# adaLN matrices of a hybrid layer: eight feature blocks summed by VectorE with the input loaded first, instead of two of them by TensorE

## The chip, the core and the metric

The kernel is written for a Trainium2 chip and runs on one of its cores. A core has a matrix engine (TensorE, PE in the profile; PEld is its weight load), VectorE (DVE), ScalarE (ACT), GpSimd (POOL) and SyncE (SP), each with its own queue of instructions that it works off in order. They work on an on-chip memory of 128 partitions; TensorE writes into accumulation banks. Transfers are issued from the queues of SyncE and ScalarE and carried by 16 DMA engines. The metric is the time of one execution on the device in microseconds (us), as the median over several runs. Engines wait for each other and for transfers by semaphores, and a transfer's semaphore is one of eight that are used in turn, so a transfer is issued once the one eight places earlier has landed.

## The reference

The model layer takes x of 2048 tokens by 1024 features and one condition vector c of 1024. What matters here is the start:

```
c_act = silu(c)
mod = c_act @ w_ada + b_ada                  # 1024 -> 6 x 1024
shift_m, scale_m, gate_m, shift_f, scale_f, gate_f = split(mod, 6)
h = rms_norm(x, g_norm_mix) * (1 + scale_m) + shift_m
p = h @ w_in                                 # 1024 -> 3592
...                                          # convolutions, gated delta rule, w_out, feed-forward, final adaLN
```

So the first projection needs, for each feature, a shift and a scale, each the dot product of c_act with a column of w_ada, and x normalised along its rows. Everything is in float32.

## The kernel before, in words

The kernel works through the 2048 tokens in four blocks of 512 (BLK), and features are split into eight feature blocks of 128 (KD). Activations stand with features on the partitions, so x is normalised token by token and then turned by TensorE transposes. To keep float32 precision, an operand of a projection is split into a high part (a cast to the fast float32 type) and a low part (the difference); a product is then three matmuls, high by high, low by high and high by low. For the weights, ScalarE makes the high part `whi` (L368) and VectorE the low part `wlo` (L370); for the activations ScalarE scales the transposed block with the per-feature scale Gm and shift Sm (L509) and casts it to `hTh` (L510), and VectorE makes `hTl` (L511).

The head, before the loop over token blocks, does this for the first 512 tokens (tiles kq, four x tiles of 128 tokens) and feature block by feature block, k = 0 to 7. For each block it needs Gm and Sm of 128 features, that is two times 128 dot products of length 1024. There are two ways in the kernel before, chosen by `AHEAD = 2`:

- Blocks 0 and 1: a separately laid out copy `w_first` of those columns is loaded with the 1024 inputs on partitions, and TensorE multiplies it with c as a column (tile `cs`, in the storage of Gf; loaded by a small transfer of its own and put through Silu): eight matmuls of one output column for each of shift and scale, L776, accumulated in a bank.
- Blocks 2 to 7: the matrix is loaded transposed, features on partitions, and VectorE multiplies each row with the broadcast row of c (tile `crow`, shown as gate_m) and sums along the row in one instruction, L439, twice per block (scale first, then shift), into columns of two small tiles `totals` (shown as ms).

Either way ScalarE then makes Gm (L782) and Sm (L783). The matrices of the blocks lie in four places, kd, vt, yah and zs, in turn, so block k + 4 is loaded when block k is summed. Beside this the head loads and splits five weight strips of w_in (four in the ring `wraw` of four buffers, the fifth in `yal`), and projects each block with all strips that are there, so that five strips are projected at the end of the head.

The order on each engine isn't the order of the program text. A planner (class Clock) records each instruction with a cost of its own and a start time, and at the end pins, engine by engine, the instructions in the order of those planned times. Small pieces of side work are released by the same planned clock. A change in the head can therefore move instructions on any engine and anywhere behind it.

Of the kernel before, what the change touches and what calls it, by code (L numbers as in the profile page):

```python
# [12 lines left out]
F32 = mybir.dt.float32  # L13
F32R = mybir.dt.float32r
AF = mybir.ActivationFunctionType
# [5 lines left out]
P = 128  # L21
D = 1024
S = 2048
KD = D // P
# [6 lines left out]
CH = BLK // P  # L31
# [180 lines left out]


@with_exitstack
def layer_kernel(ctx, tc, x, c, w_ada, c_col, w_first, cols, g_norm_final, w_in, w_ab, xt, a_log, dt_bias, w_out, w_gate_up,
                 w_down, cst, out):
    nc = tc.nc
    x, out = x[0], out[0]
    w_down = w_down[0]
    mm = nc.tensor.matmul  # L220
# [16 lines left out]
    def misc_ps():  # L237
        return pm.tile([P, 512], F32, name="pm")
# [105 lines left out]
    epsc = g0.tile([P, 1], F32, name="epsc")  # L344
# [6 lines left out]
    col, at = {}, 0  # L351
# [3 lines left out]
    gb = g0.tile([P, KD], F32, name="gb")  # L355
# [51 lines left out]
    reqs, ready, bg = requests(), deque(), deque()  # L407
# [30 lines left out]
    def sums_of(raw, row, total):  # L438
        nc.vector.scalar_tensor_tensor(raw, raw, 1.0, row, op0=ALU.mult, op1=ALU.mult, accum_out=total)  # L439
# [80 lines left out]
    Gm, Sm, Gf, Sf = (g0.tile([P, KD], F32, name=n) for n in ("Gm", "Sm", "Gf", "Sf"))  # L520
# [146 lines left out]
    with ExitStack() as actx:  # L667
        ap_ = Split(rctx, actx, {"hTh", "hTl", "kq", "kd", "vt", "zs", "E", "X", "lv", "ch", "Dg", "state"},
                    {"halo0", "halo1", "rs", "uhalo0", "uhalo1", "edge", "uedge", "et", "strict_r", "gones_r", "junkd", "nk", "nq", "sk",
                     "bk", "rq", "cb", "ab2", "sp_y", "sp_n", "sp_e", "sp_s", "sp_z", "sp_p", "g", "beta",  # L670
                     "g_hi", "g_lo", "eg", "so"})
# [66 lines left out]
        totals = [g0.tile([P, KD], F32, name="ms", bufs=2) for _ in range(2)]  # L738
# [8 lines left out]
        crow = ap_.tile([P, D], F32, name="gate_m")  # L747
        PLACES = ("kd", "vt", "yah", "zs")

        def x_load(i):  # L750
            nc.sync.dma_start(xt0[i], x[i * P:(i + 1) * P, :])
# [7 lines left out]
                    nc.scalar.activation(xt0[i - 1], xt0[i - 1], AF.Identity, scale=ss[i - 1])  # L759

        def ada_load(k):
            if k < AHEAD:
                t = ap_.tile([P, 2, KD, P], F32, name=PLACES[k % 4])
                nc.sync.dma_start(t, w_first[k])
            else:
                t = ap_.tile([P, 2, D], F32, name=PLACES[k % 4])
                nc.sync.dma_start(t, w_ada[0:2, k].rearrange("s p n -> p s n"))
            return t

        def ada_sums(k, raw):  # L770
            if k < AHEAD:
                ps = misc_ps()
                sums = [ps[:, s:s + 1] for s in range(2)]
                for s in (1, 0):
                    for i in range(KD):
                        mm(sums[s], raw[:, s, i, :], cs[:, i:i + 1], start=s == 1 and i == 0, stop=i == KD - 1,  # L776
                           skip_group_check=True)
# [4 lines left out]
            nc.scalar.activation(Gm[:, k:k + 1], sums[1], AF.Identity, scale=col["g_mix"][:, k:k + 1], bias=gb[:, k:k + 1])  # L782
            nc.scalar.activation(Sm[:, k:k + 1], sums[0], AF.Identity, bias=col["b_sm"][:, k:k + 1])  # L783

        def proj_ab(ps, ks):
            for k in ks:
# [15 lines left out]
        nc.scalar.activation(crow, crow, AF.Silu)  # L802
# [12 lines left out]
        x_norm()  # L815
        wab = g0.tile([P, KD, 8], F32, name="wab")
        nc.sync.dma_start(wab, w_ab)
# [6 lines left out]
        for k in range(KD):  # L824
            ada_sums(k, raws[k])
            ps = turned
# [36 lines left out]
        for b in range(NB):  # L863
# [389 lines left out]
            for key, c0, dstT in (("k", 2048, kT), ("q", 1536, qT), ("v", 2560, None)):  # L1253
                clock.pinned = clock.pinned or key == "k"
                for h in range(NH):
                    m = (c0 - 1536) // P + h
                    if pre:
                        w, ps = pre.pop(0)
# [3 lines left out]
                    else:  # L1262
                        w, ps = next_w(), dense_ps()
# [22 lines left out]
            for h in range(NH):  # L1286
                w = next_w()
                ps = dense_ps()
# [67 lines left out]
            for g, group in enumerate(out_groups(b)):  # L1356
                pso = {}
                for i, (n, kp, ts) in enumerate(group):
# [132 lines left out]
    jobs, sums = deque(), deque()  # L1491
# [14 lines left out]
    strips = [(hf, m) for hf in range(2) for m in range(NF)]  # L1506
    raws, Ws, acts = {}, {}, {}
# [114 lines left out]
    raw, x0 = ready.popleft()  # L1622
# [36 lines left out]
    raws, acts_d = {}, {}  # L1659
# [211 lines left out]
    for n, (g, s) in enumerate(items):  # L1871
# [9 lines left out]
        if g == 0:  # L1881
            for q in range(4):
                p = dense_ps()
# [58 lines left out]
def laid_out(v):  # L1942
    f = {n: np.asarray(a) for n, a in v.items()}
    given = {n: f[n] for n in ("x", "c")}
    ada = np.concatenate([f["w_ada"][0], f["w_ada_final"]], axis=1)
    given["w_ada"] = ada.T.reshape(8, KD, P, D)
    given["c_col"] = f["c"].reshape(KD, P).T
    given["w_first"] = ada[:, :2 * D].reshape(KD, P, 2, KD, P)[:, :, :, :AHEAD].transpose(3, 1, 2, 0, 4)
# [31 lines left out]
```

## Time and profile before

| | us |
|---|---|
| median of three runs | 2390.36 (2387.8 to 2390.41) |
| the profiled execution, its time | 2392.24 |
| its span, first to last instruction | 2390.5 |
| TensorE busy | 2324.8 (97%) |
| VectorE busy | 1739.2 (73%) |
| ScalarE busy | 1069.5 (45%) |

In the lines of the profile, a group of instructions reads: line of the kernel, engine, operation, output tile <- input tiles with their shapes, number, then busy time, mean of one in ns, and the idle time of the engine just before them with what ended it. A row of the timeline begins with its start and its duration in us. A row of the chain of waits has start, length and what filled it; the chain is followed back from the last instruction, at each step to what released it. A row of the table by stages has the stage, its length, the busy time (and number of records) of PE, PEld, DVE, ACT and POOL, the granted TensorE clock, the share of the DMA engines and GB/s. One float32 matmul of full precision, as in L776, shows as two records.

### The profile page before, as it was taken

The numbers are of one execution on the slowest core, as the hardware profiler recorded it, in microseconds if no ns is written. First come the engines' busy times: TensorE is split into PE (matmuls) and PEld (weight loads), VectorE is DVE, ScalarE is ACT, GpSimd is POOL, SyncE is SP. The second block draws the span as 40 slices with busy tenths as digits, with TensorE's granted clock in tenths as the row PEclk, the third lists the DMA queues.
The fourth block names the chain that finished last, engine by engine and source line by source line (L and its number), as shares of the span: only waits on it lengthen the run. The fifth ranks groups of instructions, "written<-read, shape, count | busy, mean of one in ns | idle before, by whom it ended". The sixth has DMA issues, their size and how long they took to land.

```text
span 2390.5 us, 30803 instructions
## 1 busy us (share of the span) xinstructions
PE 2324.8 (97%) x11167; PEld 1924.3 (81%) x11167; DVE 1739.2 (73%) x2673; ACT 1069.5 (45%) x1865; POOL 596.8 (25%) x651
## 2 busy tenths in 40 slices
PE   6999999999999999999999999999999999999997
PEld 5788778888888888887878888878888887888786
DVE  3788859785978678786665556875655668878887
ACT  4734566445744474366433334433333323322345
POOL 0331444135413461201000000000000035434447
PEclk9999999999999999999999999999999999999999
DMA  7344555534463536255753334763433374333333
GB/s 271 106 139 123 172 177 167 164 98 163 131 209 117 178 111 203 63 167 168 231 187 103 113 89 146 233 185 93 119 97 102 106 252 150 124 106 125 131 132 149
DMA packets 217842, 352.45 MB, mean 147 GB/s; under 512 B 39149, under 2 KB 131609, under 8 KB 217370
## 3 DMA queue, kind: packets, MB, share of 16 engines
q1 hardware_dynamic: 215816, 347.46, 46.2%
q0 software_dynamic: 1152, 2.10, 0.7%
q8 instruction: 87, 1.43, 0.2%
q10 hardware_dynamic: 722, 0.93, 0.1%
q14 instruction: 65, 0.53, 0.1%
HBM read 277.01 MB, written 75.52 MB: 147 GB/s over the span
## 4 chain that ended last, share of the span: by engine, by line
PE 76%; DVE 9%; DMA 6%; ACT 4%; issue 3%; POOL 2%; SPq 0%; ACTq 0%; DVEq 0%; POOLq 0%
PE pd L325 49%; PE pm L325 17%; DVE wlo L370 1%; DVE acc L1814 1%; DMA y<-xT 1%; DVE cv L1231 1%; DMA y<-in_w_ada_dram 1%; POOL wraw L1743 1%; PE pm L898 1%; DMA A12d<-y 1%; PE pm L1113 1%; PE pm L1073 1%; PE pm L1065 1%; PE pm L1179 1%; PE pm L1187 1%
## 5 line engine op out<-in xcount | busy, mean ns | idle before, releaser
L368 ACT CAST whi<-wraw 128x1024 fp32r<-128x1024 f32 x285 | 298.5, 1049 | 368.5 <-PE pd L325 164.2
L370 DVE TENSOR_TENSOR wlo<-wraw,whi 128x1024 fp32r<-128x1024 f32 x285 | 368.4, 1294 | 119.2 <-ACT whi L368 117.5
L325 PE MATMUL pd<-hTh,whi 128*128 128x512 f32 x888 | 363.9, 410 | 6.4 <-DVE edge L1268 3.0
L325 PE MATMUL pd<-hTh,wlo 128*128 128x512 f32 x888 | 349.2, 393 | 0.0
L325 PE MATMUL pd<-hTl,whi 128*128 128x512 f32 x888 | 349.1, 393 | 0.0
L325 PEld LDWEIGHTS pd<-hTh,whi 128*128 128x128 f32 x888 | 168.3, 190 | 40.0 <-issue 3.4
L1608 POOL TENSOR_TENSOR wraw<-wraw 128x1024 f32<-128x1024 f32 x2 | 5.3, 2659 | 781.5 <-DMA wraw<-in_w_down_dram 781.5
L325 PEld LDWEIGHTS pd<-hTh,wlo 128*128 128x128 f32 x888 | 168.1, 189 | 37.1 <-issue 0.2
L325 PEld LDWEIGHTS pd<-hTl,whi 128*128 128x128 f32 x888 | 168.7, 190 | 29.4
L1231 DVE SCALAR_TENSOR_TENSOR cv<-pd,pc,cv 128x511 f32<-128x511 f32 (+2 forms) x173 | 129.1, 746 | 41.7 <-ACT cv L1229 37.9
L1556 DVE TENSOR_TENSOR sg<-sg,pd 128x512 f32<-128x512 f32 x44 | 30.2, 686 | 171.9 <-PE pd L325 171.4
L1814 DVE TENSOR_TENSOR acc<-acc,pd 128x512 f32<-128x512 f32 x192 | 127.4, 679 | 24.7 <-PE pd L325 24.6
L1694 ACT CAST xh<-ra 128x640 fp32r<-128x640 f32 (+1 forms) x85 | 60.4, 721 | 183.8 <-PE pm L325 134.4
L1703 POOL TENSOR_TENSOR xl<-ra,xh 128x640 fp32r<-128x640 f32 (+1 forms) x37 | 62.5, 1688 | 143.9 <-ACT xh L1694 143.1
L1814 DVE TENSOR_TENSOR acc<-acc,pm 128x512 f32<-128x512 f32 x120 | 81.7, 681 | 19.3 <-PE pm L325 18.8
L1743 POOL TENSOR_TENSOR wraw<-wraw 128x512 f32<-128x512 f32 x40 | 69.1, 1750 | 48.7 <-DMA wraw<-in_w_down_dram 41.7
L325 PE MATMUL pd<-whi,ym 128*128 128x512 f32 x256 | 80.4, 390 | 0.0
L325 PE MATMUL pd<-A22h,whi 128*128 128x512 f32 x176 | 70.3, 400 | 6.8 <-DVE sg L1556 6.8
L1313 DVE RECIPROCAL cv<-cv 128x128 f32<-128x128 f32 x64 | 57.1, 926 | 22.3 <-ACT cv L1310 22.2
L325 PE MATMUL pm<-S1h,whi 128*128 128x512 f32 x176 | 69.2, 393 | 1.8 <-ACT whi L368 1.8
L325 PE MATMUL pm<-S1h,wlo 128*128 128x512 f32 x176 | 69.3, 394 | 0.5 <-DVE wlo L370 0.5
L325 PE MATMUL pd<-A22l,whi 128*128 128x512 f32 x176 | 69.8, 396 | 0.0
(450 smaller groups left out, 6195.5 us busy)
## 6 DMA issues: line engine op xcount, KB each, us to landing
wraw<-in_w_in_dram SPq DMA_DIRECT2D x112, 512.0 KB, 4.4
wraw<-in_w_gate_up_dram SPq DMA_DIRECT2D x88, 512.0 KB, 3.7
ra<-act SPq DMA_DIRECT2D x80, 448.0 KB, 3.6
wraw<-in_w_out_dram SPq DMA_DIRECT2D x40, 512.0 KB, 3.7
act<-S SPq DMA_DIRECT2D x80, 256.0 KB, 2.7
act<-act SPq DMA_DIRECT2D x68, 256.0 KB, 2.2
wraw<-in_w_ada_dram SPq DMA_DIRECT2D x32, 512.0 KB, 4.3
cb<-in_x_dram SPq DMA_DIRECT2D x48, 256.0 KB, 3.7
```

The source lines that it names most:

```text
L325: mm(*args, **kw)
L368: nc.scalar.copy(hi, raw)
L370: (lo_engines.popleft() if lo_engines else nc.vector).tensor_sub(lo, raw, hi.bitcast(F32))
L898: nc.tensor.transpose(ps[:, j * P:(j + 1) * P], src[:, j * P:(j + 1) * P], ident)
L1065: mm(py[:, j * P:(j + 1) * P], Mm[h][:, j, :], T[h][:, j, :], start=True, stop=True)
L1231: nc.vector.scalar_tensor_tensor(cv[:, n - t:], u[:, :BLK - n + t], taps[t], cv[:, n - t:], op0=ALU.mult, op1=ALU.add)
L1313: nc.vector.reciprocal(sy[:, qs], sy[:, qs])
L1556: nc.vector.tensor_add(s5[i], s5[i], a[i])
L1694: nc.scalar.copy(hi, raw[:, c0:c1, :])
L1703: eng.tensor_sub(lo, raw, hi.bitcast(F32))
L1743: nc.gpsimd.tensor_mul(r[:, hs], r[:, hs], gate_f[:, hs])
L1814: nc.vector.tensor_add(accs[s, u][:, ns], accs[s, u][:, ns], ps)
```

## The change

All eight feature blocks now take the second way: `w_first`, the column of c and `AHEAD` are gone, and VectorE sums the rows of every block. A Silu on eight elements of a constant column, written to a tile whose values are overwritten later, stands ahead of the Silu of the c row. On SyncE's queue the four x tiles stand first, then matrix and weight strip of blocks 0, 1 and 2 in turn, and the matrix of block 3.

```
-AHEAD = 2
...
         def ada_load(k):
-            if k < AHEAD:
-                t = ap_.tile([P, 2, KD, P], F32, name=PLACES[k % 4])
-                nc.sync.dma_start(t, w_first[k])
-            else:
-                t = ap_.tile([P, 2, D], F32, name=PLACES[k % 4])
-                nc.sync.dma_start(t, w_ada[0:2, k].rearrange("s p n -> p s n"))
+            t = ap_.tile([P, 2, D], F32, name=PLACES[k % 4])
+            nc.sync.dma_start(t, w_ada[0:2, k].rearrange("s p n -> p s n"))
             return t

         def ada_sums(k, raw):
-            if k < AHEAD:
-                ps = misc_ps()
-                sums = [ps[:, s:s + 1] for s in range(2)]
-                for s in (1, 0):
-                    for i in range(KD):
-                        mm(sums[s], raw[:, s, i, :], cs[:, i:i + 1], start=s == 1 and i == 0, stop=i == KD - 1,
-                           skip_group_check=True)
-            else:
-                sums = [t[:, k:k + 1] for t in totals]
-                for s in (1, 0):
-                    sums_of(raw[:, s], crow, sums[s])
-            nc.scalar.activation(Gm[:, k:k + 1], sums[1], ...)
-            nc.scalar.activation(Sm[:, k:k + 1], sums[0], ...)
+            sums_of(raw[:, 1], crow, totals[1][:, k:k + 1])
+            sums_of(raw[:, 0], crow, totals[0][:, k:k + 1])
+            nc.scalar.activation(Gm[:, k:k + 1], totals[1][:, k:k + 1], ...)
+            nc.scalar.activation(Sm[:, k:k + 1], totals[0][:, k:k + 1], ...)
...
         nc.scalar.dma_start(crow, c.to_broadcast([P, D]))
-        cs = Gf
-        nc.scalar.dma_start(cs, c_col)
-        nc.scalar.activation(cs, cs, AF.Silu)
+        nc.scalar.activation(totals[0], epsc.to_broadcast([P, KD]), AF.Silu)
         nc.scalar.activation(crow, crow, AF.Silu)
         nc.scalar.dma_start(c_d, crow[0:1, :])
-        raws, strips = [ada_load(0)], []
-        x_load(0)
-        x_load(1)
-        raws.append(ada_load(1))
-        x_load(2)
-        x_load(3)
-        strips.append(next(reqs)[0](w_in, 2048))
-        raws.append(ada_load(2))
-        strips.append(next(reqs)[0](w_in, 2048 + P))
+        for i in range(CH):
+            x_load(i)
+        raws, strips = [], []
+        for k in range(3):
+            raws.append(ada_load(k))
+            strips.append(next(reqs)[0](w_in, 2048 + k * P))
         raws.append(ada_load(3))
-        strips.append(next(reqs)[0](w_in, 2048 + 2 * P))
```

How the planner's order moves is seen at three places. In the changed kernel line numbers are one lower up to the head and then up to 19 lower: L782 and L783 (Gm and Sm) become L768 and L770, the projections' L325 becomes L324, the transposes' L505 becomes L504, L759 becomes L758, L482 becomes L481 and L509, L510 become L508, L509.

ScalarE from the Silu of the c row (gate_m) to the first cast hTh of the head; kq are the x tiles, ss their row sums, pm the transposed block. Before:

```order
L802 ACTIVATE gate_m<-gate_m 128x1024
L801 ACTIVATE Gf<-Gf 128x8
L482 ACTIVATE ht,ss<-kq 128x1024
L803 DMA c_d<-gate_m 1x1024
L482 ACTIVATE ht,ss<-kq 128x1024
L759 ACTIVATE kq<-kq,ss 128x1024 x2
L782 ACTIVATE Gm<-pm,gb,pc 128x1
L783 ACTIVATE Sm<-pm,pc 128x1
L482 ACTIVATE ht,ss<-kq 128x1024
L782 ACTIVATE Gm<-pm,gb,pc 128x1
L783 ACTIVATE Sm<-pm,pc 128x1
L759 ACTIVATE kq<-kq,ss 128x1024
```

and in the changed kernel:

```order
L787 ACTIVATE gate_m<-gate_m 128x1024
L481 ACTIVATE ht,ss<-kq 128x1024
L788 DMA c_d<-gate_m 1x1024
L758 ACTIVATE kq<-kq,ss 128x1024
L481 ACTIVATE ht,ss<-kq 128x1024
L758 ACTIVATE kq<-kq,ss 128x1024
L481 ACTIVATE ht,ss<-kq 128x1024
L367 CAST whi<-wraw 128x1024
L758 ACTIVATE kq<-kq,ss 128x1024 x2
L768 ACTIVATE Gm<-ms,gb,pc 128x1
L770 ACTIVATE Sm<-ms,pc 128x1
L508 ACTIVATE pm<-pm,Sm,Gm 128x512
```

Gm and Sm, which stood in the middle of the four x tiles and read TensorE's bank (pm), now stand behind all of them and read VectorE's sums (ms). The square of x tile 0 stands ahead of these rows now.

VectorE at the start of the head, from its first instruction that reads a big tile. Before:

```order
L370 TENSOR_TENSOR wlo<-wraw,whi 128x1024
L439 SCALAR_TENSOR_TENSOR yah,ms<-yah,gate_m 128x1024 x2
L511 TENSOR_TENSOR hTl<-pm,hTh 128x512
L370 TENSOR_TENSOR wlo<-wraw,whi 128x1024
L511 TENSOR_TENSOR hTl<-pm,hTh 128x512 x2
L439 SCALAR_TENSOR_TENSOR zs,ms<-zs,gate_m 128x1024 x2
L370 TENSOR_TENSOR wlo<-wraw,whi 128x1024
```

and in the changed kernel:

```order
L438 SCALAR_TENSOR_TENSOR kd,ms<-kd,gate_m 128x1024 x2
L369 TENSOR_TENSOR wlo<-wraw,whi 128x1024
L438 SCALAR_TENSOR_TENSOR vt,ms<-vt,gate_m 128x1024 x2
L510 TENSOR_TENSOR hTl<-pm,hTh 128x512
L369 TENSOR_TENSOR wlo<-wraw,whi 128x1024
L510 TENSOR_TENSOR hTl<-pm,hTh 128x512
L438 SCALAR_TENSOR_TENSOR yah,ms<-yah,gate_m 128x1024 x2
L369 TENSOR_TENSOR wlo<-wraw,whi 128x1024
L510 TENSOR_TENSOR hTl<-pm,hTh 128x512
L438 SCALAR_TENSOR_TENSOR zs,ms<-zs,gate_m 128x1024 x2
L438 SCALAR_TENSOR_TENSOR kd,ms<-kd,gate_m 128x1024
L510 TENSOR_TENSOR hTl<-pm,hTh 128x512
```

The sums of blocks 0 (kd) and 1 (vt) are new and stand first; those of block 2 (yah) now stand behind hTl of block 1, where before they stood ahead of hTl of block 0.

TensorE from its first instruction on. Before:

```order
L505 MATMUL pm<-ck,kq 128x128
L776 MATMUL pm<-Gf,kd 128x1 x16
L505 MATMUL pm<-ck,kq 128x128
L776 MATMUL pm<-Gf,vt 128x1 x12
L505 MATMUL pm<-ck,kq 128x128 x2
L776 MATMUL pm<-Gf,vt 128x1 x4
```

and in the changed kernel:

```order
L504 MATMUL pm<-ck,kq 128x128 x16
L324 MATMUL pd<-hTh,whi 128x512
L324 MATMUL pd<-hTl,whi 128x512
L324 MATMUL pd<-hTh,wlo 128x512
L324 MATMUL pd<-hTh,whi 128x512
```

The 32 matmuls of L776 are gone; the first 16 transposes stand together and the projections follow. Behind the head (from the weight cast after block 7 on) the rows of all five engines are those of before, apart from line numbers.

More of the change, by code (lines that the diff above doesn't have):

```diff
@@ L214, in layer_kernel @@
 @with_exitstack
-def layer_kernel(ctx, tc, x, c, w_ada, c_col, w_first, cols, g_norm_final, w_in, w_ab, xt, a_log, dt_bias, w_out, w_gate_up,
+def layer_kernel(ctx, tc, x, c, w_ada, cols, g_norm_final, w_in, w_ab, xt, a_log, dt_bias, w_out, w_gate_up,
                  w_down, cst, out):
@@ L761, in ada_load @@
         def ada_load(k):
-            if k < AHEAD:
-                t = ap_.tile([P, 2, KD, P], F32, name=PLACES[k % 4])
-                nc.sync.dma_start(t, w_first[k])
-            else:
-                t = ap_.tile([P, 2, D], F32, name=PLACES[k % 4])
-                nc.sync.dma_start(t, w_ada[0:2, k].rearrange("s p n -> p s n"))
+            t = ap_.tile([P, 2, D], F32, name=PLACES[k % 4])
+            nc.sync.dma_start(t, w_ada[0:2, k].rearrange("s p n -> p s n"))
             return t
         def ada_sums(k, raw):
-            if k < AHEAD:
-                ps = misc_ps()
-                sums = [ps[:, s:s + 1] for s in range(2)]
-                for s in (1, 0):
-                    for i in range(KD):
-                        mm(sums[s], raw[:, s, i, :], cs[:, i:i + 1], start=s == 1 and i == 0, stop=i == KD - 1,
-                           skip_group_check=True)
-            else:
-                sums = [t[:, k:k + 1] for t in totals]
-                for s in (1, 0):
-                    sums_of(raw[:, s], crow, sums[s])
-            nc.scalar.activation(Gm[:, k:k + 1], sums[1], AF.Identity, scale=col["g_mix"][:, k:k + 1], bias=gb[:, k:k + 1])
-            nc.scalar.activation(Sm[:, k:k + 1], sums[0], AF.Identity, bias=col["b_sm"][:, k:k + 1])
+            sums_of(raw[:, 1], crow, totals[1][:, k:k + 1])
+            sums_of(raw[:, 0], crow, totals[0][:, k:k + 1])
+            nc.scalar.activation(Gm[:, k:k + 1], totals[1][:, k:k + 1], AF.Identity,
+                                 scale=col["g_mix"][:, k:k + 1], bias=gb[:, k:k + 1])
+            nc.scalar.activation(Sm[:, k:k + 1], totals[0][:, k:k + 1], AF.Identity, bias=col["b_sm"][:, k:k + 1])
         def proj_ab(ps, ks):
@@ L1946, in laid_out @@
     given["w_ada"] = ada.T.reshape(8, KD, P, D)
-    given["c_col"] = f["c"].reshape(KD, P).T
-    given["w_first"] = ada[:, :2 * D].reshape(KD, P, 2, KD, P)[:, :, :, :AHEAD].transpose(3, 1, 2, 0, 4)
     b_ada, b_fin = f["b_ada"].reshape(-1, P), f["b_ada_final"].reshape(-1, P)
```

## The prediction

> **What bounds the kernel now.** I read the page first: its busy times, its forty slices and its chain of work.
>
> ```profile
> span 2390.5 us, 30803 instructions
> PE 2324.8 (97%) x11167; PEld 1924.3 (81%) x11167; DVE 1739.2 (73%) x2673; ACT 1069.5 (45%) x1865; POOL 596.8 (25%) x651
> PE   6999999999999999999999999999999999999997
> PE 76%; DVE 9%; DMA 6%; ACT 4%; issue 3%; POOL 2%; SPq 0%; ACTq 0%; DVEq 0%; POOLq 0%
> ```
>
> TensorE (PE) is busy in every slice but the first and the last, and three quarters of the chain is its own work. So whatever lets TensorE begin its real work earlier should shift all that follows, and the first slice (0 to 60 us) is the place of the change. There I read the chain in order of time.
>
> ```profile
> 2.14 10.70 DMA Gf<-in_c_col_dram
> 13.41 0.74 ACT ht L482 x3
> ...
> 15.14 1.07 ACT kq L759
> ...
> 16.73 6.62 PE pm L776 x32
> ...
> 23.67 4.91 PE pm L776 x24
> ...
> 29.11 1.51 PE pm L776 x8
> ...
> 34.16 1.16 ACT kq L759
> ```
>
> The chain starts with the 4 KB column c, which lands at 12.84, goes through two normalised x tiles and then through the 64 records of L776: TensorE summing feature blocks 0 and 1, one column at a time. They hold the chain for 6.62 + 4.91 + 1.51 = 13.04 us. ScalarE (ACT) is meanwhile stuck: Gm and Sm of block 0 wait for these sums, and the third and fourth x tiles stand behind Gm and Sm in ScalarE's queue. VectorE (DVE) does nothing at all. The timeline shows this, the first projection, and the end of the stretch:
>
> ```profile
> 10.40 1.06 ACT L802 ACTIVATE gate_m<-gate_m 128x1024 f32<-128x1024 f32 x1 [6.09 <-DMA gate_m<-in_c_dram]
> 12.97 1.04 ACT L482 ACTIVATE ht<-kq 128x1024 bf16<-128x1024 f32 x1
> 13.92 0.19 ACT L482 ACTIVATION_READ_ACCUMULATOR ht<-kq 128x1 f32 x1
> 14.20 0.19 POOL L476 TENSOR_SCALAR ss<-ss 128x1 f32<-128x1 f32 x1 [12.79 <-ACT ht L482]
> 14.47 0.56 POOL L477 TENSOR_TENSOR ss<-ss,mhalf 128x1 f32<-128x1 f32 x1
> 23.39 0.35 ACT L782 ACTIVATE Gm<-pm,gb,pc 128x1 f32<-128x1 f32 x1 [6.14 <-PE pm L776]
> 23.64 0.25 ACT L783 ACTIVATE Sm<-pm,pc 128x1 f32<-128x1 f32 x1
> 34.18 1.23 DVE L370 TENSOR_TENSOR wlo<-wraw,whi 128x1024 fp32r<-128x1024 f32 x1 [26.48 <-ACT whi L368]
> 35.87 1.42 ACT L509 ACTIVATE pm<-pm,Sm,Gm 128x512 f32<-128x512 f32 x2 [0.56 <-PE pm L505]
> 36.47 1.22 DVE L439 SCALAR_TENSOR_TENSOR yah<-yah,gate_m 128x1024 f32<-128x1024 f32 x1
> 37.21 1.07 ACT L510 CAST hTh<-pm 128x512 fp32r<-128x512 f32 x2
> 37.86 0.80 PE L325 MATMUL pd<-hTh,whi 128*128 128x512 f32 x1 [1.38 <-ACT hTh L510]
> 71.73 1.05 ACT L368 CAST whi<-wraw 128x1024 fp32r<-128x1024 f32 x1 [3.40 <-PE pd L325]
> ```
>
> The first projection starts at 37.86. The weight cast at 71.73 waits for the last block's matmuls, so I take it as the end of the head: 33.87 us after the first projection.
>
> **The change part by part.** Two numbers decide: when the first projection can start, and whether the 33.87 us after it stay.
>
> *What no longer holds the start.* The 64 records of L776 are gone (13.04 us of the chain), and so are the small transfer of c as a column and its Silu. Blocks 0 and 1 now cost VectorE four sums of 1.22 us. They lie in its idle 26.48 us, provided their data are there. The table load of Silu, which a tiny activation now pulls forward, and the store of c lie beside waits too. So I work out the loads.
>
> ```profile
> 0.00:5.00 5.00, 0.00 (x0) 0.00 (x0) 0.52 (x4) 1.28 (x1) 0.87 (x7) 1.00 0.63 211
> 5.00:10.00 5.00, 0.00 (x0) 0.00 (x0) 0.17 (x1) 0.00 (x0) 0.00 (x0) 1.00 1.00 386
> 10.00:15.00 5.00, 0.00 (x0) 0.00 (x0) 0.00 (x0) 3.20 (x6) 0.72 (x2) 1.00 1.01 413
> 60.00:70.00 10.00, 10.00 (x50) 7.86 (x49) 3.62 (x6) 5.20 (x11) 0.24 (x1) 1.00 0.01 2
> ```
>
> The last column is GB/s. By 5 us 1.06 MB have moved, by 10 us 2.99 MB, then 0.413 MB per us. SP now brings four x tiles of 0.52 MB (2.10 MB), then the matrices of block 0 (1.05 MB), a weight strip (0.52), block 1 (1.05) and so on; beside them ScalarE's queue moves 0.66 MB (identity, columns, c row). All x is in by about 9.5 us. Block 0 is complete at 2.10 + 0.66 + 1.05 = 3.81 MB, so at 10 + 0.82 / 0.413 = 12.0; the strip at 13.3; block 1 at 15.8; block 2 at 19.6. VectorE sums block 0 from 12.0 to 14.4 and block 1 after the first strip's low half: neither is last. I leave the landing of the c row at 10.40, since its queue has one transfer less behind it and none less ahead.
>
> *The new chain to the first projection* is then ScalarE's own queue in its new order. From 10.40: Silu of the c row 1.06; squares of x tiles 1 to 3, 3 x (1.04 + 0.19) = 3.69 (that of tile 0 runs earlier, while the c row is still on its way); GpSimd's 0.19 + 0.56 once, before the first scaling; four scalings at 1.14 (4.56; the chain shows 1.07 and 1.16); one weight cast 1.05 (as at 71.73); Gm and Sm 0.60, beside which TensorE's last transposes run; the scaling of block 0, 1.42 / 2 = 0.71; Gm of block 1, which now stands between, 0.35; the cast hTh, 1.07 / 2 = 0.54. The sum is 13.31, so the first projection starts at 23.7 instead of 37.86: **14.1 us earlier**. Bounds: every queue step could cost 0.1 more in hand-over (15 steps, 1.5 us less), or the c row could land up to 2 us sooner.
>
> *The 33.87 us after it.* TensorE has the same matmuls there. VectorE has more to do per block than before only in total: from the first projection on, six pairs of sums (14.6), three low halves and the fifth strip's (4.9) and eight hTl (0.69 each by the row below, 5.5) make 25.0 us. Before, the last hTl began at 68.37, 3.4 us ahead of the end of the head.
>
> ```profile
> L511 DVE TENSOR_TENSOR hTl<-pm,hTh 128x512 fp32r<-128x512 f32 x8 | 5.5, 692 | 8.3 <-ACT hTh L510 8.1
> 68.37 0.69 DVE L511 TENSOR_TENSOR hTl<-pm,hTh 128x512 fp32r<-128x512 f32 x1 [3.51 <-ACT hTh L510]
> 39.88 0.63 PE L325 MATMUL pd<-hTl,whi 128*128 128x512 f32 x1
> 40.30 0.63 PE L325 MATMUL pd<-hTh,wlo 128*128 128x512 f32 x1
> 45.10 0.39 PE L325 MATMUL pd<-hTh,wlo 128*128 128x512 f32 x1
> 45.33 0.40 PE L325 MATMUL pd<-hTh,whi 128*128 128x512 f32 x1
> ```
>
> So VectorE must deliver the last hTl by 23.7 + 33.87 - 3.4 = 54.2, and has 54.2 - 23.7 = 30.5 us for 25.0 us of work: some 5.5 us may go in waits. Early on it is tighter. Blocks 2 and 3 each need a pair of sums, a low half and an hTl, 4.4 us, and these stand in a row with a trip to ScalarE between; TensorE has 15 matmuls for block 2, 3.4 us at the later pace. It will stand idle for a microsecond or so at blocks 2 and 3. Against that, TensorE's start is slow anyway: its steps are 0.42 us at 39.88 and 0.23 at 45.10, and idle time inside a slow spell is partly made good. The bounds are 0 and 2.5 us lost; I take 1.0, nearer the low end because of the 5.5 us.
>
> The Trainium skill speaks against the change here. "TensorE: Matmul & The Clock Gate", section "HAM oscillation — how this bites in real kernels", says that idle gaps beyond about 3.4 us halve TensorE's clock again. Two such relapses between blocks would cost, as an estimate from that page, 2 x 1.7 = 3.4 us and leave a gain of about 10. The trace agrees in kind (a slow start, released about 5 us in); whether gaps of the length I expect, about 1 us, slow it again, no row of before shows.
>
> *What follows the head* hangs on it. Row by row, past the head all five engines' orders are those of before. The loads have nothing to catch up with: DMA moved 2 GB/s at 60 to 70 us, and the strips ahead wait for buffers that the head frees. So a shift reaches the end in full, or nearly.
>
> The sum: 14.1 - 1.0 = **13.1 us** off. The profiled execution took 2392.24 (span 2390.5), so it would be 2379.1; that execution lay 1.9 above the median of the runs, so the median goes from 2390.36 to about **2377.3**.
>
> **The rivals.** *VectorE becomes the pace.* If each block's sums, trip to ScalarE and hTl ran strictly in a row, a block would take 2.44 + 0.60 + 0.71 + 0.54 + 0.69 = 5.0 us, eight 39.8, and with five low halves (6.2) 46.0: from 12.0 to 58.0. Block 7's matmuls and the rest of block 6 would end the head about 6 us later, at 64 to 66, and the gain is 6 to 8: 2382 to 2385. For it: in the new order the sums of block 2 stand right behind the hTl of block 1. Against it: a sum of block 4 stands ahead of block 3's hTl, those of block 7 ahead of block 6's, and elsewhere the low halves fill most of the trip.
>
> *The gain is lost after the head.* The stretch to 100 us has VectorE in the chain, and if something there waited for a transfer and not for the head, the shift would end there: 2388 to 2391. For it speaks only that the stretch isn't TensorE's; against it, the 2 GB/s.
>
> *Slower, by TensorE's slow pace.* If the holes between blocks kept it at 0.42 instead of 0.23 for all 105 projection matmuls of blocks 0 to 6 and some 14 small ones, that is 119 x 0.19 = 23 us, of which some 5 us / 0.42 x 0.19 = 2.3 us were paid before; against 14.1 saved, the kernel ends 6 to 7 us slower, 2397. It decides once slow steps number more than some 74 beyond those of before. Against it: a slow TensorE falls behind VectorE, so it has no more holes, and 5 us without holes ended the slow spell before.
>
> That the change doesn't do what it says I can leave out: the two sets of TensorE sums are absent from its order, and the x loads stand first.
>
> **How the numbers follow.** The forecast (2374 to 2381) has 0.72; VectorE as the pace 0.16; lost after the head 0.08; slower 0.04. Some 0.01 of the second would miss 0.2% (4.8 us, about what this measurement can tell from no change; the three runs lie within 2.6). So faster 0.87, same 0.09, slower 0.04. The range runs from 2373.5 (c row sooner, no hole) to 2384.5, and takes in most of the second case.
>
> **What would show it.** The first projection near 24 and the weight cast that waits for the last block near 58.7 would bear out both terms. A first projection above 27 means that the c row or the x tiles came late; a head longer than 37 us with idle TensorE in front of hTl means VectorE; with matmul steps of 0.42 past 35 us, the slow pace. A head 13 us shorter with a span less than 10 us shorter would make the last step wrong.

## The result and the profile after

| | before | after |
|---|---|---|
| median of six runs each, us | 2389.86 (2387.8 to 2394.71) | 2375.88 (2374.11 to 2379.62) |
| ratio, 95% interval | | 0.9942 (0.9929 to 0.9955) |
| the profiled execution: time, span | 2392.24, 2390.5 | 2376.71, 2374.9 |
| first projection starts at | 37.86 | 22.51 |
| weight cast that ends the head, at | 71.73 | 56.32 |

The change made the kernel faster by 14.0 us of medians; 2377.3 was forecast, with a range of 2373.5 to 2384.5. The profiled executions differ by 15.6 us of span, and 15.4 of these are there at the end of the head.

The page of the changed kernel has the same look as that of before, with the first slice still at 6 (first the busy us, share and number of instructions of each engine, then the busy tenths of TensorE in 40 slices):

```profile
span 2374.9 us, 30687 instructions
PE 2310.0 (97%) x11103; PEld 1910.2 (80%) x11103; DVE 1745.8 (74%) x2681; ACT 1070.6 (45%) x1865; POOL 596.8 (25%) x651
PE   6999999999999999999999999999999999999997
```

What changed is inside that first slice. The timeline of the changed kernel (start, duration, and in brackets the idle time ahead with its releaser) shows the new start and the end of the head:

```profile
9.98 1.06 ACT L787 ACTIVATE gate_m<-gate_m 128x1024 f32<-128x1024 f32 x1 [4.03 <-DMA gate_m<-in_c_dram]
13.02 1.15 ACT L758 ACTIVATE kq<-kq,ss 128x1024 f32<-128x1024 f32 x1 [0.94 <-POOL ss L476]
13.55 1.23 DVE L438 SCALAR_TENSOR_TENSOR kd<-kd,gate_m 128x1024 f32<-128x1024 f32 x1 [6.79 <-DMA kd<-in_w_ada_dram]
18.12 2.18 ACT L758 ACTIVATE kq<-kq,ss 128x1024 f32<-128x1024 f32 x2
20.21 0.37 ACT L768 ACTIVATE Gm<-ms,gb,pc 128x1 f32<-128x1 f32 x1
22.51 0.80 PE L324 MATMUL pd<-hTh,whi 128*128 128x512 f32 x1 [1.04 <-ACT hTh L509]
29.20 0.50 PE L324 MATMUL pd<-hTh,wlo 128*128 128x512 f32 x1 [0.85 <-DVE wlo L369]
34.53 0.96 PE L324 MATMUL pd<-hTh,whi 128*128 128x512 f32 x3 [0.23 <-ACT hTh L509]
56.32 1.05 ACT L367 CAST whi<-wraw 128x1024 fp32r<-128x1024 f32 x1 [3.39 <-PE pd L324]
```

From the landing of the c row on, ScalarE works almost without a pause up to the first cast hTh (its one long wait is 0.94 us for GpSimd), and the first projection starts at 22.51, so 15.35 us earlier. VectorE begins its sums of block 0 at 13.55, when their matrix lands. Their totals are read at 20.21, 4.3 us after the last sum ended (14.70 + 1.22), so the sums are not on the path. From the first projection to the weight cast it takes 56.32 - 22.51 = 33.81 us, against 33.87 before.

That equal length has two parts, which the table by stages shows (length, then busy time of PE, PEld, DVE, ACT and POOL, granted clock, share of the DMA engines, GB/s). The stretch in the kernel before:

```profile
37.86:71.73 33.87, 33.24 (x140) 25.16 (x141) 22.23 (x33) 17.61 (x34) 1.11 (x2) 1.00 0.41 139
```

and in the changed kernel:

```profile
22.51:56.32 33.81, 32.73 (x140) 24.45 (x141) 24.32 (x37) 19.00 (x37) 0.57 (x2) 1.00 0.64 241
```

TensorE's idle time grew from 0.63 to 1.08 us: the holes at blocks 2 and 3 are there, 0.85 and 0.23 us. Its busy time fell by 0.51 us, because the slow spell at the start was shorter: the matmuls of the timeline reach their later duration of 0.39 to 0.40 us at 26.80, 4.3 us after the first projection, and at 44.63, 6.8 us after it, in the kernel before. This spell has to be read from the records (0.63 us against 0.39): the granted clock stands at 1.00 in the table all the same.

One sentence ahead of the prediction was too wide: the planner pins the order of the instructions only behind the head. In the head the order comes from the scheduler of the kernel's framework, which works from the program text and costs of its own; so some experiments below moved instructions that their edit did not name.

### The profile page after: what moved, and what is told of

It reads as the page before. It is cut to its first block, busy times and chain, and to the rows that moved or that the text cites. A ratio compares the mean times of both kernels' runs of the same rounds, so it can differ in the third digit from the quotient of the medians.

```text
span 2374.9 us, 30687 instructions
## 1 busy us (share of the span) xinstructions
PE 2310.0 (97%) x11103; PEld 1910.2 (80%) x11103; DVE 1745.8 (74%) x2681; ACT 1070.6 (45%) x1865; POOL 596.8 (25%) x651
## 5 line engine op out<-in xcount | busy, mean ns | idle before, releaser
L324 PE MATMUL pd<-hTh,whi 128*128 128x512 f32 x888 | 362.6, 409 | 5.6 <-DVE edge L1249 3.0
L324 PE MATMUL pd<-hTh,wlo 128*128 128x512 f32 x888 | 348.9, 393 | 0.9 <-DVE wlo L369 0.9
L324 PE MATMUL pd<-hTl,whi 128*128 128x512 f32 x888 | 348.6, 393 | 0.0
L324 PEld LDWEIGHTS pd<-hTh,whi 128*128 128x128 f32 x888 | 167.8, 189 | 38.7 <-issue 3.4
L324 PEld LDWEIGHTS pd<-hTh,wlo 128*128 128x128 f32 x888 | 167.8, 189 | 38.2 <-DVE wlo L369 1.5
L324 PEld LDWEIGHTS pd<-hTl,whi 128*128 128x128 f32 x888 | 168.5, 190 | 30.0 <-DVE hTl L510 0.4
L324 PE MATMUL pd<-whi,ym 128*128 128x512 f32 x256 | 80.4, 390 | 0.0
L324 PE MATMUL pd<-A22h,whi 128*128 128x512 f32 x176 | 69.5, 395 | 4.2 <-DVE sg L1537 4.2
L324 PE MATMUL pm<-S1h,whi 128*128 128x512 f32 x176 | 68.7, 390 | 1.3 <-ACT whi L367 1.3
L324 PE MATMUL pm<-S4h,whi 128*128 128x512 f32 x176 | 68.6, 390 | 1.1 <-ACT sg L1531 1.1
L324 PE MATMUL pd<-S3h,t3h 128*128 128x512 f32 x176 | 69.0, 392 | 0.6 <-ACT sg L1523 0.6
```

The source lines that it names most:

```text
L324: mm(*args, **kw)
```

## The experiments

All start from the changed kernel unless said otherwise. Positions are from one profiled execution each, in us; the ratio is to the kernel before on the same chip.

| | first projection | end of head | head after its start | ratio, 95% interval |
|---|---|---|---|---|
| before | 37.86 | 71.73 | 33.87 | |
| the change | 22.51 | 56.32 | 33.81 | 0.9942 (0.9929 to 0.9955) |
| sums moved, loads as before | 27.54 | 61.06 | 33.52 | 0.9962 (0.9949 to 0.9974) |
| loads moved, sums as before | 33.26 | 65.79 | 32.53 | 0.9980 (0.9964 to 0.9995) |
| one block by TensorE | 25.82 | 58.54 | 32.72 | 0.9942 (0.9922 to 0.9962) |
| sums of blocks 0, 1 twice | 22.83 | 57.66 | 34.83 | 0.9952 (0.9939 to 0.9965) |
| Silu of the c row later | 20.47 | 54.31 | 33.84 | 0.9925 (0.9908 to 0.9941) |
| c row loaded first | 20.43 | 56.59 | 36.16 | 0.9944 (0.9927 to 0.9961) |
| the change again | 22.31 | 56.12 | 33.81 | 0.9945 (0.9928 to 0.9961) |
| sums of blocks 2, 3 twice | 22.36 | 59.11 | 36.75 | one run, 2378.18 us |
| sums of blocks 6, 7 twice | 22.54 | 56.51 | 33.97 | one run, 2375.5 us |

**Half the change: VectorE sums every block, but the loads stand in their old order.**

```diff
-        for i in range(CH):
-            x_load(i)
-        raws, strips = [], []
-        for k in range(3):
-            raws.append(ada_load(k))
-            strips.append(next(reqs)[0](w_in, 2048 + k * P))
+        raws, strips = [ada_load(0)], []
+        x_load(0)
+        x_load(1)
+        raws.append(ada_load(1))
+        x_load(2)
+        x_load(3)
+        ...                                   # then strip, matrix 2, strip
         raws.append(ada_load(3))
+        strips.append(next(reqs)[0](w_in, 2048 + 2 * P))
```

> VectorE sums all eight blocks as in the change, but the loads stand in the order of before (matrix 0, x 0 and 1, matrix 1, x 2 and 3, strip, ...). My theory (ScalarE's queue up to the first cast sets the start, and the start sets the end): ScalarE now meets x 2 and 3 only behind Gm and Sm of block 0 and 1, so the first projection comes at 24.5 to 26 instead of 22.5 us, the weight cast that ends the head at 58 to 60 instead of 56.3, and the kernel takes 1.5 to 3.5 us more than the change, some 12 less than before. Rival (the gain is the load order's): the start falls back to 33 or later and less than 5 us of the gain is left.

The head ended 10.7 us earlier than before and 4.7 later than with the change. Where the 4.7 us go, ScalarE's rows in this kernel's timeline tell:

```profile
12.26 1.06 ACT L481 ACTIVATE ht<-kq 128x1024 bf16<-128x1024 f32 x1 [0.56 <-ACT gate_m L787]
15.69 1.15 ACT L758 ACTIVATE kq<-kq,ss 128x1024 f32<-128x1024 f32 x1 [0.97 <-POOL ss L476]
18.17 0.28 ACT L770 ACTIVATE Sm<-ms,pc 128x1 f32<-128x1 f32 x1
18.35 0.37 ACT L768 ACTIVATE Gm<-ms,gb,pc 128x1 f32<-128x1 f32 x1
18.63 1.04 ACT L481 ACTIVATE ht<-kq 128x1024 bf16<-128x1024 f32 x1
20.71 1.15 ACT L758 ACTIVATE kq<-kq,ss 128x1024 f32<-128x1024 f32 x1 [0.76 <-POOL ss L476]
```

The square of the third x tile runs at 18.63, where the changed kernel is already at its last two scalings (18.12). The square of tile 0 runs only behind the c row, at 12.26 (4.80 in the change, where x is loaded first); Gm and Sm of blocks 0 and 1 stand among the x tiles; and three of the four scalings wait for GpSimd (0.97, 0.27 and 0.76 us), in the change only one. So the loads' order is worth 4.7 us of the 15.4, by the order of ScalarE's queue that comes with it. The forecast of 24.5 to 26 for the first projection missed by 1.5 us, that of 58 to 60 for the end of the head by 1.1.

**The other half: only the loads' order, TensorE still sums blocks 0 and 1.** The kernel before, with the loads of the change (the lines with a minus above, put back in).

> Only the load order of the change (four x tiles first), with blocks 0 and 1 still summed by TensorE. My theory: the 64 records of TensorE (13.0 us) can't start before matrix 0 lands at 13.5, and the scaling of block 0 stands behind Gm of block 1 in ScalarE's queue, so the first projection comes at 28 to 32 us, the head ends at 62 to 66, and the kernel is 6 to 9 us faster than before and 6 to 9 slower than the change. Rival (load order alone): first projection near 22.5, the whole gain of 14. Rival (engine alone): within 2 us of before.

```profile
12.43 0.21 ACT L801 ACTIVATE Gf<-Gf 128x8 f32<-128x8 f32 x1 [5.31 <-DMA Gf<-in_c_col_dram]
30.63 0.35 ACT L782 ACTIVATE Gm<-pm,gb,pc 128x1 f32<-128x1 f32 x1 [7.28 <-PE pm L776]
```

These are ScalarE's rows of that kernel. The column of c still holds ScalarE until 12.43, and the second Gm stands ahead of the first scaling and waits 7.28 us for TensorE's one-column matmuls. The head ended 5.9 us earlier than before, at 65.79 and so within the expected 62 to 66; the first projection, at 33.26, came 1.3 us later than the 28 to 32 expected. By the ratio the kernel is 4.8 us faster than before (interval 1.2 to 8.6; 6 to 9 expected). The two halves alone give 10.7 and 5.9 of the 15.4 us: they add up nearly, with 1.2 us counted twice.

**One block by TensorE, one by VectorE** (`AHEAD = 1`, x loaded first).

> Load order of the change, block 0 summed by TensorE, block 1 by VectorE. My theory: TensorE's 32 records for block 0 (6.8 us) run from 13.5 to 20.3, just while ScalarE still works on the x tiles until 20.3, so they are hidden: first projection at 22 to 23.5, end of the head within 1 us of the change (56.3), the kernel within 1 us of it. Rival (sums by TensorE cost their time wherever they stand): 6 to 7 us slower than the change.

The end of the head came 2.2 us later than with the change, not within 1, and the first projection at 25.82, not at 22 to 23.5: the scaling of block 0 stands at 23.57 and waited for transposes which TensorE had behind its 32 one-column records.

```profile
21.49 0.35 ACT L782 ACTIVATE Gm<-pm,gb,pc 128x1 f32<-128x1 f32 x1 [1.05 <-PE pm L776]
23.57 0.75 ACT L509 ACTIVATE pm<-pm,Sm,Gm 128x512 f32<-128x512 f32 x1 [1.58 <-PE pm L505]
```

The time cannot be told from that of the change (0.9942 both). TensorE's sums cost the path even for a single block.

**VectorE doubled in blocks 0 and 1.** The first pair of sums writes its products to a tile that is free then, its totals are overwritten with the same values by the second pair.

```diff
         def ada_sums(k, raw):
+            if k < 2:
+                for s in (1, 0):
+                    nc.vector.scalar_tensor_tensor(spare, raw[:, s], 1.0, crow, op0=ALU.mult, op1=ALU.mult,
+                                                   accum_out=totals[s][:, k:k + 1])
...
+        spare = ap_.tile([P, D], F32, name="yal")
```

> The change, with the four sums of blocks 0 and 1 done twice on VectorE (the first result is overwritten by the second): 4.9 us more work for VectorE at the start. My theory: VectorE has some 5 us to spare until the last hTl, so only what falls on blocks 0 and 1 shows: first projection at 22.5 to 23.5, end of the head 0.5 to 2.5 us later than in the change (56.3). Rival (VectorE sets the pace of the head): the end of the head 4.5 to 5 us later, and the kernel with it.

Of 4.9 us more on VectorE 1.34 reached the end of the head, 0.32 of them by the first projection. So the sums of the first two blocks lie for the most part in VectorE's waiting time, as the change needs.

**VectorE doubled in blocks 2 and 3, and in blocks 6 and 7.** The same edit with `k in (2, 3)` and with `k in (6, 7)`, and the products to a tile of half width (bf16). A few of VectorE's rows changed places with it.

> The change, with the sums of blocks 2 and 3 done twice (the first pair of each writes its products to a spare tile, and its totals are overwritten by the second pair with the same values): 4 x 1.22 = 4.9 us more on VectorE, right behind the first projections, where TensorE had its two holes (0.85 and 0.23 us). Theory A, that of the prediction (VectorE has some 5.5 us to spare between the first projection and the last hTl): the head, 33.81 us from first projection to weight cast, grows by no more than 1 us. Theory B (VectorE's chain of sums, trip to ScalarE and hTl is the pace from block 2 on, with nothing to spare): it grows by 4.5 to 5. Between them: the early blocks have no reserve, but TensorE has work of the later strips to fall back on: 1.5 to 3.5, which is what I expect.

> The same 4.9 us more on VectorE, but in the sums of blocks 6 and 7, where VectorE stood 3.5 us before the last hTl. By rows of the change the sums of block 7 end at 48.1, and the scaling of block 7 waits for TensorE's transposes until 51.55; with 4.9 us more the sums end at 53.0, 1.5 after that. Theory A (5.5 us to spare over all): the head grows by 0 to 0.5 us. My expectation from the rows: 1 to 2.5. Theory B (VectorE the pace up to the end): 4.5 to 5.

The table by stages for the stretch from the first projection to the end of the head, blocks 2 and 3 doubled:

```profile
22.36:59.11 36.75, 34.31 (x140) 24.97 (x141) 28.66 (x45) 18.87 (x36) 1.34 (x2) 1.00 0.60 221
```

and blocks 6 and 7 doubled:

```profile
22.54:56.51 33.97, 33.57 (x140) 24.79 (x141) 28.59 (x45) 19.18 (x36) 1.43 (x2) 1.00 0.64 238
```

VectorE's busy time (the third figure) is the same in both, 28.6 against 24.32 in the change. Early, it costs 2.9 us, within the 1.5 to 3.5 expected; late, 0.2. So the reserve of VectorE is at the end of the head, and there is little at its start. The changed kernel's own rows of VectorE and ScalarE show why:

```profile
25.03 0.69 DVE L510 TENSOR_TENSOR hTl<-pm,hTh 128x512 fp32r<-128x512 f32 x1 [0.37 <-ACT hTh L509]
26.90 0.39 ACT L768 ACTIVATE Gm<-ms,gb,pc 128x1 f32<-128x1 f32 x1 [0.95 <-DVE yah L438]
28.37 0.75 ACT L508 ACTIVATE pm<-pm,Sm,Gm 128x512 f32<-128x512 f32 x1
29.77 0.69 DVE L510 TENSOR_TENSOR hTl<-pm,hTh 128x512 fp32r<-128x512 f32 x1 [0.63 <-ACT hTh L509]
34.51 0.69 DVE L510 TENSOR_TENSOR hTl<-pm,hTh 128x512 fp32r<-128x512 f32 x1 [0.62 <-ACT hTh L509]
47.21 0.75 ACT L508 ACTIVATE pm<-pm,Sm,Gm 128x512 f32<-128x512 f32 x1 [0.86 <-PE pm L504]
51.55 0.75 ACT L508 ACTIVATE pm<-pm,Sm,Gm 128x512 f32<-128x512 f32 x1 [0.92 <-PE pm L504]
```

The loop of VectorE and ScalarE (sums, Gm and Sm, scaling, hTh, hTl) takes 4.74 us per block for blocks 2 and 3, and nothing in it waits for TensorE. At blocks 6 and 7 the scaling waits for TensorE's transposes: TensorE is behind, and the two scalings are 4.34 us apart. The two paces are close to each other, and this is my reading of why the holes stay so small. My first expectation for blocks 6 and 7 (1 to 2.5) was too high. I had let the end of the head move with the sums of block 7, but TensorE had other matmuls to do until their hTl came, at 55.09: its idle time in that kernel is 0.40 us, less than in the change.

**Is the start really ScalarE's queue?** If so, an instruction taken out from behind the c row must move the start. The Silu of the c row stands ahead of the squares of x tiles 1 to 3; in this kernel it stands in the text with the scalings, and the framework put it behind the square of tile 1.

```diff
         def x_norm():
...
+                if i == 2:
+                    nc.scalar.activation(crow, crow, AF.Silu)
+                    nc.scalar.dma_start(c_d, crow[0:1, :])
                 if i:
                     nc.scalar.activation(xt0[i - 1], xt0[i - 1], AF.Identity, scale=ss[i - 1])
...
-        nc.scalar.activation(crow, crow, AF.Silu)
-        nc.scalar.dma_start(c_d, crow[0:1, :])
```

> The change, with one instruction of ScalarE's queue moved: the Silu of the c row (1.06 us) stands behind the squares of x tiles 1 and 2 instead of ahead of them. My theory (the start is the sum of ScalarE's queue, counted from the landing of the c row at 9.98): the square of tile 1 (0.95) then runs before the c row has landed, and the wait for GpSimd ahead of the first scaling (0.94) is covered by the Silu and the square of tile 2. First projection at 20.4 to 21.0 instead of 22.5; the sums of VectorE start no later, since matrix 0 lands at 13.55. If all of it reaches the end of the head, the weight cast that waits for block 7 comes at 54 to 55 instead of 56.3 and the kernel is about 2 us faster than the change. Rival: VectorE and the loads set the pace behind the start; then the first projection is as early, but the cast comes at 56 to 56.5 and the time is that of the change.

```profile
6.08 1.06 ACT L481 ACTIVATE ht<-kq 128x1024 bf16<-128x1024 f32 x1 [0.28 <-DMA kq<-in_x_dram]
10.02 1.06 ACT L758 ACTIVATE gate_m<-gate_m 128x1024 f32<-128x1024 f32 x1 [2.79 <-DMA gate_m<-in_c_dram]
12.02 2.17 ACT L761 ACTIVATE kq<-kq,ss 128x1024 f32<-128x1024 f32 x2
20.47 0.79 PE L324 MATMUL pd<-hTh,whi 128*128 128x512 f32 x1 [1.04 <-ACT hTh L509]
54.31 1.05 ACT L367 CAST whi<-wraw 128x1024 fp32r<-128x1024 f32 x1 [3.40 <-PE pd L324]
```

This is the timeline of that kernel. The square of tile 1 now runs at 6.08, in the time that ScalarE spends waiting for the c row; the scalings start at 12.02 instead of 13.02 and without the wait for GpSimd. Start and end of the head both come 2.0 us earlier than in the change (1.8 against its repeat on the same chip). The median is 2370.98 us, 4.4 below the repeat's 2375.34. The two intervals overlap, so of the whole time only this much is shown: it is faster than the kernel before by 0.6 to 0.9%. That it is faster than the change by about 2 us rests on the head. Its median and its ratio are the lowest of this study.

**The c row loaded first.** If the landing of the c row starts the sum, an earlier landing should pay too.

```diff
-        nc.scalar.dma_start(crow, c.to_broadcast([P, D]))
+        nc.sync.dma_start(crow, c.to_broadcast([P, D]))
```

> The change, with the c row (0.52 MB) loaded first on SyncE's queue, ahead of the four x tiles, instead of beside them on ScalarE's queue. My theory: the c row is in by about 4.5 instead of 9.98, each x tile about 1.3 later, and ScalarE's queue begins with the data of the x tiles; the first projection comes at 18.5 to 20 instead of 22.5. Then matrix and sums of block 0 (landed at 13.5, 2.4 us of sums, 16.0) are not yet in the way, but block 1's matrix (about 17) and the loads behind it are near: I expect the end of the head only 1.5 to 3.5 us earlier, the cast at 53 to 55, and the kernel 1.5 to 3.5 us faster than the change. Rival 1 (the start alone sets the end): cast at 52.3 to 53.8. Rival 2 (VectorE and the loads set the end): cast at 56 or later.

The timeline of that kernel, ScalarE's and VectorE's rows in order of time:

```profile
5.45 1.06 ACT L787 ACTIVATE gate_m<-gate_m 128x1024 f32<-128x1024 f32 x1 [2.30 <-DMA gate_m<-in_c_dram]
16.41 1.15 ACT L758 ACTIVATE kq<-kq,ss 128x1024 f32<-128x1024 f32 x1 [1.54 <-POOL ss L476]
20.41 0.69 DVE L510 TENSOR_TENSOR hTl<-pm,hTh 128x512 fp32r<-128x512 f32 x1 [0.37 <-ACT hTh L509]
22.27 0.39 ACT L768 ACTIVATE Gm<-ms,gb,pc 128x1 f32<-128x1 f32 x1 [1.90 <-DVE vt L438]
25.23 0.69 DVE L510 TENSOR_TENSOR hTl<-pm,hTh 128x512 fp32r<-128x512 f32 x1 [0.37 <-ACT hTh L509]
30.05 0.69 DVE L510 TENSOR_TENSOR hTl<-pm,hTh 128x512 fp32r<-128x512 f32 x1 [0.37 <-ACT hTh L509]
56.59 1.05 ACT L367 CAST whi<-wraw 128x1024 fp32r<-128x1024 f32 x1 [3.40 <-PE pd L324]
```

The c row landed 4.5 us earlier and the first projection came 2.1 us earlier (the last x tile was scaled at 16.41, after a wait of 1.54 us for GpSimd), but the end of the head did not move (0.3 later). GpSimd's two small instructions for that tile took 0.96 and 1.42 us, beside VectorE's sums of block 0; for the tile before they took 0.19 and 0.55. My expectation of 1.5 to 3.5 us was wrong, and the second rival right in its first half, VectorE: the sums of block 1 followed on VectorE's other work without waiting for their matrix. In this order the hTl of block 0 stands ahead of the sums of block 1, so the loop of VectorE and ScalarE, 4.82 us per block, runs from block 0 on. In the change the sums of block 1 are done before the first projection, and hTl of blocks 0 and 1 are 2.5 us apart (22.49 and 25.03). hTl of block 1 comes at 25.23 here and at 25.03 in the change; from there on both go at about the same pace. So a gain at the start counts only if the sums of block 1 move with it, as they did with the later Silu (18.49 was the start of their last one, against 20.54).

**The change again, on the chip of the last two kernels.**

> The changed kernel itself, unaltered, beside the two variants on the same chip: 2373 to 2379, 0.994 of the kernel before (0.993 to 0.9955). Its stretch to the first projection (22.5) and to the weight cast (56.3) should repeat within 0.5 us, while the span behind the head may differ by several us from one execution to the next, as in the kernels profiled so far (2309.9 to 2323.9).

It repeats: 2375.34 us, the head to 0.2 us. TensorE's slow spell ended 5.1 us after the first projection instead of 4.3, and the head after its start is 33.81 in both: the loop of VectorE and ScalarE was the pace there, and the longer slow spell took the place of the hole at block 2 (0.28 us instead of 0.85).

## Why the prediction was right, and where its sizes were off

- **The start (14.1 us earlier forecast, 15.35 measured).** The chain was the one foretold, link by link: c row, squares, GpSimd once, four scalings, one weight cast, Gm and Sm, scaling, Gm of block 1, hTh. The term was mis-sized twice, both times to the cautious side. The c row landed at 9.98, not 10.40. And the queue sum was 12.53 us (22.51 - 9.98), not 13.31: I had added up durations, but rows that follow each other without a wait start up to 0.1 us before the end of the one before (two scalings together are 2.18, not 2 x 1.14). The bound "0.1 more in hand-over" had the wrong sign. The lower end of the range, 2373.5, is 0.8 us below what its own two bounds give (14.1 + 2.0 off, 2374.3); the measured median lies above both. The kernel with the later Silu shows by intervention that this queue is the path.
- **The loads.** Matrix 0 was forecast for 12.0 and landed at 13.55. Somewhat less had moved by 10 us than I took from before (2.79 MB, not 2.99), and my reckoning by bytes took SyncE's queue to be served strictly in order. By 13.55 the transfers had moved, by the table by stages of the changed kernel below, 5 x 0.189 + 5 x 0.369 + 3.55 x 0.419 = 4.28 MB, where 3.81 would have completed block 0. The missing 0.47 MB are most likely the strip behind it, issued at 4.80 on the same queue, which moved beside it; that was not tried apart. It cost nothing, since Gm read the sums at 20.21.

```profile
0.00:5.00 5.00, 0.00 (x0) 0.00 (x0) 0.52 (x4) 1.69 (x3) 0.87 (x7) 1.00 0.64 189
5.00:10.00 5.00, 0.00 (x0) 0.00 (x0) 0.17 (x1) 0.97 (x3) 0.19 (x1) 1.00 1.01 369
10.00:13.55 3.55, 0.00 (x0) 0.00 (x0) 0.00 (x0) 2.61 (x4) 1.27 (x3) 1.00 1.03 419
```

- **The holes (1.0 us forecast, -0.06 measured).** The holes were foretold at blocks 2 and 3 and stand there, 1.08 us in all. What I had wrong is what they cost: idle time grew by only 0.45 us, since before had its own 0.63, and the slow spell gave 0.51 back. "Partly made good" was wholly made good, and some of that is luck: the slow spell of before, in the one execution that I have of it, is the longest of all those profiled (4.0 to 6.8 us).
- **VectorE's spare time (5.5 us forecast).** As a total it holds: 24.32 us of work in the stretch, where 25.0 were forecast. As a single number it misleads. The doubled sums show 0.2 us lost of 4.9 late in the head, 2.9 early, 1.3 ahead of the first projection. The rival "VectorE becomes the pace" was true for blocks 2 and 3 (4.74 us per block, its working said 5.0) and false for the head, because TensorE with five strips needs nearly as long per block (4.34 us between the scalings of blocks 6 and 7, which wait for it) and ends last.
- **The shift reaches the end.** Borne out: head 15.4 us shorter, median 14.0 (interval 10.8 to 17.0). That the one pair of spans gives 15.6 is luck, since the stretch behind the head took from 2309.9 to 2323.9 us in the executions profiled. In the kernels with four or more runs the change of the head lies within the interval of the change of the time: 10.7 for the first half (6.2 to 12.2), 5.9 for the second (1.2 to 8.6).
- **The clock.** Neither the 2397 of a TensorE that stays slow nor the two relapses that would have left a gain of about 10 took place in the changed kernel. Holes of 0.85 us and of 1.26 us (blocks 2 and 3 doubled) were each followed by matmul records of 0.39 to 0.50 us, not of 0.63. But the rival was nearer than that: in the kernel with one block by TensorE, TensorE was at full pace for its first two projection matmuls (0.73 us for both), and behind pauses of 1.21 and 0.64 us it was slow again for 3.4 us, at a granted clock of 0.51. So holes of about 1 us can do it, when two of them fall close together. A relapse costs 1.6 us by the last section, close to the 1.7 that the prediction estimated.

```profile
25.82 0.73 PE L325 MATMUL pd<-hTh,whi 128*128 128x512 f32 x2 [1.21 <-ACT hTh L510]
27.19 0.50 PE L325 MATMUL pd<-hTl,whi 128*128 128x512 f32 x1 [0.64 <-DVE hTl L511]
27.77:31.22 3.45, 3.45 (x12) 2.81 (x12) 3.39 (x6) 2.42 (x5) 0.00 (x0) 0.51 1.03 420
```

## What to carry to other kernels

When work is taken from one engine to another, write down the new order of the queue that then ends last and add it up from the landing that starts it; here that gave the start of the first projection to within 1.3 us. An engine's spare time is not one number: ask at which block it stands, and check it by doubling work early and late. A start that comes earlier pays only if the work of the next blocks moves with it.

## What the runs showed of the hardware

**A pause of 3.0 us can make TensorE slow, and whether it does differs between executions of one program.** Behind the head, TensorE waits 3.0 us for VectorE in every one of these kernels. The changed kernel, the matmul behind that pause and the five us from it on by stage:

```profile
69.86 0.47 PE L324 MATMUL pd<-hTh,whi 128*128 128x512 f32 x1 [3.02 <-DVE edge L1249]
69.86:74.86 5.00, 5.00 (x15) 3.99 (x16) 4.93 (x7) 2.56 (x6) 2.76 (x2) 0.66 0.60 181
```

and the same program in its second profiled execution:

```profile
69.66 0.47 PE L324 MATMUL pd<-hTh,whi 128*128 128x512 f32 x1 [3.03 <-DVE edge L1249]
69.66:74.66 5.00, 5.00 (x22) 4.14 (x23) 4.93 (x7) 2.56 (x6) 2.77 (x2) 1.00 0.48 169
```

In the first, the granted clock of those 5 us is 0.66 and 15 matmuls are done; in the second 1.00 and 22. The slow spell costs 7 x 0.23 = 1.6 us of TensorE's time. It came in 8 of the 11 profiled executions, with pauses of 3.00 to 3.04 us; the other three had pauses of 3.00 to 3.03 us, and each of the three chips of the experiments shows both. What differs is where the pause falls. In every trace the changes of the granted clock lie a whole number of 3.41 us apart. The changed kernel's stretch of that length ahead of the fall and the slow one, and in the second execution the two stretches over which the pause is spread:

```profile
67.22:70.64 3.42, 0.78 (x4) 0.67 (x5) 3.35 (x6) 1.65 (x3) 3.42 (x5) 1.00 0.89 295
70.64:74.05 3.41, 3.41 (x10) 2.67 (x9) 3.34 (x7) 1.00 (x4) 1.98 (x1) 0.50 0.42 82
```

```profile
64.92:68.33 3.41, 1.72 (x8) 1.10 (x6) 3.34 (x4) 2.82 (x7) 3.41 (x3) 1.00 0.24 91
68.33:71.74 3.41, 2.08 (x9) 1.76 (x10) 3.41 (x5) 1.93 (x4) 3.41 (x4) 1.00 0.57 216
```

TensorE was idle for 2.6 us of the first stretch, and for 1.7 and 1.3 us of the two in the second execution. Over all eleven traces, each of the 59 falls of the granted clock came at the end of such a stretch with 1.6 us or more of idle, and every stretch at full clock with more than 1.92 us was followed by one; in between it went either way. The Trainium skill, "TensorE: Matmul & The Clock Gate", section "HAM oscillation — how this bites in real kernels", sets the limit at gaps of about 3.4 us; the measurement decides, and 3.0 as the profile counts them (3.39 to 3.43 from the start of one matmul to the start of the next) were enough here, in some executions and not in others. The same page's section "What's actually happening" says that the window in which activity is watched runs freely, so that the same kernel meets it at different phases. The traces agree: the first slow spell ended 4.3 and 5.1 us after the first projection in two executions of the changed kernel, and from 4.0 to 6.8 us over the ten executions whose projections began slow, with 7 to 12 projection matmuls before its end.

**One execution says little about the rest.** Behind the head the same program took 2374.9 - 56.32 = 2318.6 us in one execution and 2371.4 - 56.12 = 2315.3 in another, at mean granted clocks of 0.993 and 0.996. So a gain of 2 us is read from the position of a row in the head, which repeats to 0.2 us, and not from one span.
